# One VectorE instruction for three closing half rows, GpSimd's last products into tiles already stored, and new order tables for every engine

## The chip, the core and the metric

The kernel runs on one core of one Trainium2 chip. The metric is the device time of one execution in microseconds (us), lower is better. One execution was also taken with the hardware profiler, and every duration below comes from that trace.

## What is computed

One decoder layer with four head groups, 1024 tokens by 1024 channels, in float32. Cut to what matters here:

```python
h = rms_norm(x, norm_g)
p = h @ w_in                                  # 1024 x 3652
y_fox = forgetting_attention(fq, fk, fv, log_f)
y_sb  = stick_breaking_attention(sq, sk, sv)
y_rw  = rwkv7_time_mix(rw, ...)               # a recurrence over the tokens
y_lru = rg_lru(lx, ...)
y = concat(y_fox*silu(fg), y_sb*silu(sg), y_rw*silu(rg), y_lru*silu(lg))
x = x + y @ w_out
return x * rsqrt(mean(x*x) + eps) * final_g   # the final RMSNorm
```

## The kernel before, in words

TensorE (PE in the profile) is the engine that matters: float32 products are made from float32r pieces (a rounded high part and a low rest), so each product of the projections and of the output is three matmuls of 128x512 (names `xh`/`xl`, `wh`/`wl`, `woh`/`wol`).

The program runs in stages that overlap:

- From 0 to about 300 us: the input projections (`pj_...`, line L402, later L989) and, woven between their matmuls, the RWKV group. Its recurrence is cut into chunks of 64 tokens, and each chunk is a chain across engines (L758): `px` on PE, `X` on ACT, `pu` and `py` on PE, `UV` on DVE, `ph` on PE, and so on. Between two links of this chain PE works on projection matmuls, which thus are the filling of the gaps. Earlier, a low-rank gate of RWKV runs through `rbc` (a row of scales is spread over the partitions), tanh on ACT and the small matmuls `pw`/`pa` (L498, L501), and a norm over heads through `pn` (L518).
- From about 300 to 470 us: the stick-breaking attention (names ending in `sb`) with the remaining projections as filling.
- From about 470 to 594 us: the forgetting attention (`fox`). Scores `zfox` (L1174) go into PSUM banks; VectorE (DVE) reads a bank, adds the bias and writes `atfox` with a running maximum `mx` (L1213); `nb` (L1218, L1219) is the negated maximum; ScalarE (ACT) takes the exponential (L1222) and scales it by the reciprocal of the sum (L1226, L1229); PE transposes (`ptfox`, L1246), ACT and DVE split the result into `PHfox` and `PLfox` (L1251, L1252), and PE multiplies with the values `VS` (`avfox`, L1256). The filling here is the output projection over three of the four head groups: for row tile `tt` and column half `n` a PSUM tile `po` takes 18 matmuls (L1351) of the weights `woh`/`wol` and of `yc`, the mixed outputs of two row tiles, and one DVE addition (L1353) writes `ac = po + xt`. GpSimd (POOL) issues the loads of `yc` (L1403, two of 768 KB for each pair of tiles), of the residual rows `xt` (L1409, 256 KB each, two buffers), of raw weights `wor` (L1331), and the stores `p_fv` (L1006) of the value projections. In `po<tt><n>` and `xt<tt><n>` the two figures are tile and column half; `yc<g><n>` serves the tiles 2g and 2g+1.
- From 594 us on: the fox group's part of the output (`pofx`, 96 matmuls, L1351), added to `ac` by DVE, and the final RMSNorm by row tile in `out_norm`, in the order 6, 7, 4, 5, 2, 3, 0, 1: ACT squares a half row with its sum (L1359), DVE and ACT make the reciprocal root `rs` (L1361 to L1374), POOL multiplies the half row by the weight `fg` (L1381) in place, and ACT (L1385) or, for three last half rows, DVE (L1383) scales it by `rs`; then it is stored (L1386).

The order of work on each engine is written out by hand: `ORDERS` holds for each of the five engines a list of instruction numbers, and `in_order` lays each engine's stream out by it. A DMA is queued by the engine that issues it: POOL's DMAs go out in the order of POOL's stream, between its own instructions. Each engine works off its stream strictly in order, so an instruction that waits holds all behind it.

Of the kernel before, what the change touches and what calls it, by code (L numbers as in the profile page):

```python
# [13 lines left out]
ALU = mybir.AluOpType  # L14
# [28 lines left out]
for _name, _w in (  # L43
# [171 lines left out]
def tile_hybrid_trunk(ctx: ExitStack, tc: tile.TileContext, a, dbg=None):  # L215
    nc = tc.nc
# [12 lines left out]
    HELD = {}  # L229
# [850 lines left out]
    QB = 2  # L1080
# [274 lines left out]
    def out_norm(w1, op, ac, fg, tt, last):  # L1355
# [21 lines left out]
        for n in range(2):  # L1377

            cs = slice(n * HS, (n + 1) * HS)
# [171 lines left out]
```

## Time and profile before

| | us |
|---|---|
| median of 3 runs | 627.14 (626.68 to 628.49) |
| the profiled execution | 629.03 |
| its span in the trace | 627.1 |
| PE busy | 608.5 (97%), 4060 records |
| DVE busy | 489.8 (78%) |
| ACT busy | 390.7 (62%) |
| POOL busy | 200.8 (32%) |
| granted TensorE clock, mean | 0.992 |

The span is the trace's time from the first to the last event; the execution's own time is 1.9 us longer. Read the table so: PE is busy nearly all the time, so a microsecond is won only where PE idles or runs at a lower clock, or behind its last matmul at 617.14 us.

### The profile page before, as it was taken

Reading aid. Unit: us, or ns where it says so; the run is one execution under the profiler, and the core shown is the slowest. Engines: PE = TensorE matmul, PEld = TensorE weight load, DVE = VectorE, ACT = ScalarE, POOL = GpSimd, SP = SyncE. Lnnn points to the kernel's source line nnn. Section 1 sums busy time; section 2 is a strip of 40 time slices with the busy share of each in tenths; the row PEclk is TensorE's granted clock in tenths of the full one; section 3 lists DMA queues with packets and bytes.
Section 4 is the critical chain, followed back from the end, with each engine's and each line's share of the span. In section 5 each row is a group of like instructions: output and inputs, shape, how many; then the busy total and the mean of one; then the engine's idle time right before and its main releaser. Section 6 shows DMA issues by size and latency. Waiting matters only on the chain.

```text
span 627.1 us, 11831 instructions
## 1 busy us (share of the span) xinstructions
PE 608.5 (97%) x4060; PEld 494.9 (79%) x4060; DVE 489.8 (78%) x1131; ACT 390.7 (62%) x722; POOL 200.8 (32%) x328
## 2 busy tenths in 40 slices
PE   8999999999999999999999999999999999999993
PEld 6867777778876687777888888879997788888882
DVE  6598687998996796978866988888774776857687
ACT  6797948451013378797534776567764657766575
POOL 2231421313113675444343220400223222322175
PEclk9999999999999999999999999999999899999997
DMA  8873766527351336721998665355498867763225
GB/s 288 305 220 87 193 176 152 143 101 183 108 165 62 103 99 222 241 100 71 254 300 270 202 211 159 134 169 168 143 273 298 261 207 248 256 197 135 84 102 201
DMA packets 86403, 114.35 MB, mean 182 GB/s; under 512 B 38151, under 2 KB 57927, under 8 KB 86344
## 3 DMA queue, kind: packets, MB, share of 16 engines
q1 hardware_dynamic: 69112, 57.81, 31.0%
q0 software_dynamic: 16656, 55.23, 26.1%
q8 instruction: 32, 0.52, 0.3%
q10 hardware_dynamic: 576, 0.56, 0.3%
q14 instruction: 27, 0.22, 0.1%
HBM read 79.31 MB, written 33.21 MB: 179 GB/s over the span
## 4 chain that ended last, share of the span: by engine, by line
PE 65%; DVE 13%; ACT 7%; DMA 7%; issue 6%; POOL 2%; SPq 1%; DVEq 0%; ACTq 0%; POOLq 0%
PE po L1351 9%; PE pj_fk L402 4%; PE pofx L1351 4%; PE pj_sg L402 4%; PE pj_fq L402 3%; PE pj_sq L402 3%; PE pj_rg L402 3%; PE pj_fg L402 3%; PE zsb L1174 3%; PE avfox L1256 3%; PE pj_v L402 3%; PE zfox L1174 2%; PE avsb L1256 2%; PE ptfox L1246 2%; DMA xr<-in_xT_dram 2%
## 5 line engine op out<-in xcount | busy, mean ns | idle before, releaser
L1351 PE MATMUL po<-woh,yc 128*128 128x512 f32 x192 | 69.6, 412 | 0.0
L1190 DVE TENSOR_TENSOR_SCAN atsb<-kp,atsb 128x128 f32<-128x128 f32 (+7 forms) x32 | 43.4, 1362 | 5.1 <-ACT atsb L1188 4.9
L1351 PE MATMUL po<-wol,yc 128*128 128x512 f32 x96 | 39.8, 414 | 0.0
L1222 ACT ACTIVATE atfox<-atfox,nb 128x128 f32<-128x128 f32 (+7 forms) x32 | 24.6, 770 | 23.9 <-DVE nb L1219 12.7
L1351 PEld LDWEIGHTS po<-woh,yc 128*128 128x128 f32 x192 | 34.8, 192 | 2.9
L1187 ACT ACTIVATE kp<-zsb 128x512 f32<-128x512 f32 (+3 forms) x48 | 23.6, 491 | 17.5 <-PE zsb L1174 17.0
L1252 DVE TENSOR_TENSOR PLfox<-ptfox,PHfox 128x512 fp32r<-128x512 f32 (+1 forms) x40 | 25.4, 636 | 10.4 <-ACT PHfox L1251 9.8
L1252 DVE TENSOR_TENSOR PLsb<-ptsb,PHsb 128x512 fp32r<-128x512 f32 (+1 forms) x40 | 25.1, 630 | 8.3 <-ACT PHsb L1251 7.5
L1251 ACT ACTIVATE PHsb<-ptsb 128x512 fp32r<-128x512 f32 (+1 forms) x40 | 22.1, 555 | 10.8 <-PE avsb L1256 5.9
L1251 ACT ACTIVATE PHfox<-ptfox 128x512 fp32r<-128x512 f32 (+1 forms) x40 | 21.9, 548 | 11.1 <-PE avfox L1256 9.7
L1174 PE MATMUL zsb<-KSsb,Q 128*128 128x512 f32 (+3 forms) x96 | 28.6, 357 | 0.0
L1174 PE MATMUL zfox<-KSfox,Q 128*128 128x512 f32 (+3 forms) x96 | 25.6, 349 | 2.2 <-DVE mx L1213 2.2
L1229 ACT ACTIVATE atfox<-atfox,sm 128x128 f32<-128x128 f32 (+7 forms) x32 | 23.4, 767 | 0.7 <-DVE sm L1226 0.7
L1188 ACT ACTIVATE atsb<-zsb 128x512 f32<-128x512 f32 (+3 forms) x48 | 23.4, 488 | 0.0
L749 POOL TENSOR_TENSOR Hp<-UV,PC 64x128 f32<-64x128 f32 x32 | 16.6, 518 | 21.3 <-DVE UV L796 17.6
L1174 PEld LDWEIGHTS zfox<-KSfox,Q 128*128 128x128 f32 x96 | 17.8, 191 | 6.2 <-DVE mx L1213 2.6
L1246 PE MATMUL ptsb<-ident,atsb 128*128 128x128 f32 x144 | 22.2, 272 | 0.4 <-DVE PLsb L1252 0.4
L1381 POOL TENSOR_TENSOR ac<-ac,fg 128x512 f32<-128x512 f32 x16 | 20.7, 1324 | 5.6 <-ACT ot L1359 5.6
L1213 DVE CUSTOM_DVE_ANT_0 atfox<-zfox,Fb 128x512 f32<-128x512 f32 (+3 forms) x40 | 20.9, 524 | 2.0 <-PE zfox L1174 1.8
L1246 PEld LDWEIGHTS ptfox<-ident,atfox 128*128 128x128 f32 x144 | 18.2, 140 | 5.5
L1246 PE MATMUL ptfox<-ident,atfox 128*128 128x128 f32 x144 | 22.2, 272 | 0.0
L1256 PE MATMUL avsb<-PLsb,VS 128*128 128x256 f32 x80 | 20.1, 286 | 0.9 <-DVE PLsb L1252 0.7
(547 smaller groups left out, 2161.6 us busy)
## 6 DMA issues: line engine op xcount, KB each, us to landing
yc<-yx_d POOLq DMA_DIRECT2D x16, 768.0 KB, 6.9
xn<-in_x_dram SPq DMA_DIRECT2D x8, 512.0 KB, 5.3
Q<-p_sq SPq DMA_DIRECT2D x64, 64.0 KB, 3.4
Q<-p_fq SPq DMA_DIRECT2D x64, 64.0 KB, 3.6
xt<-in_x_dram POOLq DMA_DIRECT2D x16, 256.0 KB, 6.1
out_dram<-ac SPq DMA_DIRECT2D x15, 256.0 KB, 2.1
xr<-in_xT_dram SPq DMA_DIRECT2D x6, 512.0 KB, 9.0
wor<-in_w_out_dram SPq DMA_DIRECT2D x9, 256.0 KB, 3.8
```

The source lines that it names most:

```text
L402: mm = nc.tensor.matmul(out[0:ww.shape[-1]], ww, xx[hf][:, k], start=(k == 0 and xx is xh and ww is wh), stop=(k == KT - 1 and ww is wl))
L1174: ((hi - c) / 2400, nc.tensor.matmul(z[:, c - lo:hi - lo], q, k, start=j == 0, stop=j == len(ops) - 1))
L1187: nc.scalar.activation(kp[:, lo:hi], z[:, 0:hi - lo], AF.Sigmoid, scale=-0.125)
L1188: nc.scalar.activation(at[:, lo:hi], z[:, 0:hi - lo], AF.Sigmoid, scale=0.125)
L1190: nc.vector.tensor_tensor_scan(rv, kp[:, 0:n][:, ::-1], rv, 0.0, op0=ALU.mult, op1=ALU.add)
L1222: exp = nc.scalar.activation(At[qb][:, 0:n], At[qb][:, 0:n], AF.Exp, bias=nb[:, qb:qb + 1], scale=0.125, accum_out=sm_[:, 0, qb:qb + 1])
L1229: nc.scalar.activation(At[qb][:, 0:n], At[qb][:, 0:n], AF.Copy, scale=sm_[:, 1, qb:qb + 1])
L1246: T.append((P / 1200, nc.tensor.transpose(pt[:, col:col + P], At[qb][:, (2 * m + j) * P:(2 * m + j + 1) * P], ident)))
L1251: nc.scalar.activation(PH[:, 0:w], pt[:, 0:w], AF.Copy)
L1252: nc.vector.tensor_tensor(PL[:, 0:w], pt[:, 0:w], PH[:, 0:w], op=ALU.subtract)
L1256: V.append(((c1 - c0) / 2400, nc.tensor.matmul(av[:, q0:256], VS[:, 2 * m + j, :], pp[:, c0:c1], start=m == 0 and j == 0 and pi == 0, stop ...
L1351: mm = nc.tensor.matmul(po, y, w, start=i == 0, stop=i == len(ops) - 1)
```

## The change

`out_norm` multiplies the three half rows that VectorE finishes (half 1 of tile 3, half 1 of tile 0, half 0 of tile 1) by `rs` and by `fg` in one scalar_tensor_tensor, where before GpSimd multiplied by `fg` and VectorE scaled by `rs`. GpSimd thus has 13 products in place of 16. For the tiles 0 and 1 the results, of both engines, go into the tiles `ac4` and `ac5`, which were stored before, rather than in place.

All tables in `ORDERS` are new. The table of PE is the same from about its 2260th instruction on (from about 340 us); the tables of DVE, ACT, POOL and SP differ in places throughout. Since DVE's table is one line longer, a line number of the changed kernel is one more than that of the same code before.

```diff
     "PE": (
-        "0-9 14-25 38-49 26-37 50-93 10-13 94-109 150-161 110 111 162-197 112 198-221 258-283 117-123 125-131 124 "
+        "0-9 14-25 38-49 26-37 50-87 10-13 88-103 110 111 104-109 150-175 112 176-219 117-123 125-131 124 132-136 "
...
@@ -1377,11 +1378,11 @@
         for n in range(2):
 
             cs = slice(n * HS, (n + 1) * HS)
-            yn = ac[tt][:, cs]
-            nc.gpsimd.tensor_tensor(yn, yn, fg[:, cs], op=ALU.mult)
+            y, yn = ac[tt][:, cs], ac[tt + 4 if tt < QB else tt][:, cs]
             if n in last:
-                HELD[f"scaled{tt}"] = nc.vector.tensor_scalar_mul(yn, yn, rs)
+                HELD[f"scaled{tt}"] = nc.vector.scalar_tensor_tensor(yn, y, rs, fg[:, cs], op0=ALU.mult, op1=ALU.mult)
             else:
+                nc.gpsimd.tensor_tensor(yn, y, fg[:, cs], op=ALU.mult)
                 HELD[f"scale{tt}"] = nc.scalar.activation(yn, yn, AF.Copy, scale=rs)
             (nc.scalar if tt == 1 and n in last else nc.sync).dma_start(a["out"][tt * P:(tt + 1) * P, cs], yn)
```

Three places of the new order follow, each as it stood and as it stands.

**POOL around the first residual row, at about 467 to 475 us.** The names: `FM11` is a mask tile, `yc10` the mixed outputs of the tiles 2 and 3, `xt00` and `xt10` the residual rows of tile 0 and 1, `p_fv` the stored value projections, `wor51` and `wor61` raw output weights. Before:

```order
L1331 DMA wor51_5641<-in_w_out_dram 128x512
L1331 DMA wor61_5647<-in_w_out_dram 128x512
L1006 DMA p_fv_2720<-sp_fv6_2950 128x512
L1197 AFFINE_SELECT FM11_6115<-Fb1_5960 128x256
L1403 DMA yc10_5582<-yx_d_128 128x6x256 x2
L1409 DMA xt00_5538<-in_x_dram 128x512
L1006 DMA p_fv_2720<-sp_fv7_2980 128x512
L1409 DMA xt10_5560<-in_x_dram 128x512
```

After:

```order
L1007 DMA p_fv_2720<-sp_fv6_2950 128x512
L1198 AFFINE_SELECT FM11_6115<-Fb1_5960 128x256
L1410 DMA xt00_5538<-in_x_dram 128x512
L1404 DMA yc10_5582<-yx_d_128 128x6x256 x2
L1410 DMA xt10_5560<-in_x_dram 128x512
L1007 DMA p_fv_2720<-sp_fv7_2980 128x512
```

The load of `xt00` stands ahead of the two large loads of `yc10` where it stood behind them; the two raw weights left this place (they now follow the load of `xt50`), and `xt10` changed places with the last store.

**DVE around the first addition of `po` and `xt`, at about 480 to 488 us.** The names: `nb11` is the negated maximum for which ACT's exponentials of `atfox12` and `atfox13` wait; `atfox04` and `atfox05` are scores on their way out of the PSUM banks `zfox`; `mx` is a running maximum, `sm` a sum of exponentials. Before:

```order
L1353 TENSOR_TENSOR ac0_5527<-po00_5540,xt00_5538 128x512
L1218 TENSOR_REDUCE nb11_6134<-mx11_6119 128x2
L1219 TENSOR_SCALAR nb11_6134<-nb11_6134 128x2
L1201 MEMSET mx12_6263 128x6
L1226 RECIPROCAL sm_11_6121<-sm_11_6121 128x2
L1213 ISA atfox04_6187,mx02_6184<-zfox040_6188,Fb0_5950 128x512
...
L1252 TENSOR_TENSOR PLfox010_6090<-ptfox010_6084,PHfox010_6089 128x512
```

After:

```order
L1219 TENSOR_REDUCE nb11_6134<-mx11_6119 128x2
L1220 TENSOR_SCALAR nb11_6134<-nb11_6134 128x2
L1202 MEMSET mx12_6263 128x6
L1262 TENSOR_TENSOR ypfox00_5963<-avfox10_6031,ypfox00_5963 64x256
L1214 ISA atfox04_6187,mx02_6184<-zfox040_6188,Fb0_5950 128x512
...
L1253 TENSOR_TENSOR PLfox010_6090<-ptfox010_6084,PHfox010_6089 128x512
L1354 TENSOR_TENSOR ac0_5527<-po00_5540,xt00_5538 128x512
```

The addition stood ahead of `nb11` and of the reading of the next score bank and now stands behind both; the reciprocal, which waits for the exponentials, no longer stands ahead of `atfox04`.

**PE in the second chunk of the RWKV chain, at about 185 to 188 us.** `pu`, `py` and `ph` are links of the chain, `pj_sq` the projection that fills. Before:

```order
L758 MATMUL py_3341<-UV_256,TR_259 64x64 x2
L402 MATMUL pj_sq_0_1571<-xh_126,wh_sq_1_1566 128x512
L402 MATMUL pj_sq_0_1571<-xl_127,wh_sq_1_1566 128x512
L402 MATMUL pj_sq_0_1571<-xh_126,wl_sq_1_1567 128x512
L402 MATMUL pj_sq_0_1571<-xh_126,wh_sq_1_1566 128x512
L402 MATMUL pj_sq_0_1571<-xl_127,wh_sq_1_1566 128x512
L758 MATMUL ph_3385<-UV_256,BKT_260 64x64 x4
```

After:

```order
L759 MATMUL py_3341<-UV_256,TR_259 64x64 x2
L403 MATMUL pj_sq_0_1571<-xl_127,wh_sq_0_1560 128x512
L403 MATMUL pj_sq_0_1571<-xh_126,wl_sq_0_1561 128x512
L403 MATMUL pj_sq_0_1571<-xh_126,wh_sq_1_1566 128x512
L759 MATMUL ph_3385<-UV_256,BKT_260 64x64 x4
```

Three filling matmuls stand between `py` and `ph` where five stood. Of the first eight chunks, five now have just three there; before, one had.

199 rows, old and new, of the table ORDERS are left out of this document.

## The prediction

> **What bounds the kernel now.** The page comes first: who is busy, and what clock TensorE was granted in 40 slices of the span.
>
> ```profile
> PE 608.5 (97%) x4060; PEld 494.9 (79%) x4060; DVE 489.8 (78%) x1131; ACT 390.7 (62%) x722; POOL 200.8 (32%) x328
> PEclk9999999999999999999999999999999899999997
> ```
>
> PE leaves 18.6 us of 627.1 idle, so a change in the order of the other engines pays only where PE idles or is slowed, or behind PE's last matmul. The clock falls once in mid program, in slice 32 (486 to 502 us), and otherwise only in the last slice. Next, the table of PE's waits, with total, count and longest:
>
> ```profile
> PE zfox L1174 <- DVE mx L1213: 2.2, 1, 2.2
> PE pn L518 <- ACT N L516: 0.8, 1, 0.8
> PE ph L758 <- DVE UV L783: 0.7, 3, 0.3
> PE avsb L1256 <- DVE PLsb L1252: 0.7, 1, 0.7
> ```
>
> One wait stands out, 2.2 us before a score matmul, and it lies just where the clock falls. The chain of waits between 440 and 500 us says what it hangs on (start, duration, what):
>
> ```profile
> 473.34 10.46 DMA xt<-in_x_dram
> 483.83 0.69 DVE ac L1353
> 484.83 1.42 ACT atfox L1222 x4
> 486.44 0.59 DVE atfox L1213
> 487.09 1.22 PE zfox L1174 x2
> ```
>
> The load of the first residual row took 10.46 us. DVE's addition waited for it, and behind the addition stood the maximum `nb11` for ACT's exponentials, behind these (through the reciprocal) DVE's reading of a score bank, and behind that PE's next scores. The timelines of POOL, DVE and PE give the pieces; the bracket at a row's end is the idle time before it and what ended it:
>
> ```profile
> 467.77 1.08 POOL L1331 DMA_DIRECT2D wor<-in_w_out_dram  x2
> 471.66 1.70 POOL L1403 DMA_DIRECT2D yc<-yx_d  x2 [1.20 <-PE zfox L1174]
> 473.34 0.56 POOL L1409 DMA_DIRECT2D xt<-in_x_dram  x1
> 483.83 0.69 DVE L1353 TENSOR_TENSOR ac<-po,xt 128x512 f32<-128x512 f32 x1 [3.16 <-DMA xt<-in_x_dram]
> 484.49 0.40 PE L1351 MATMUL po<-wol,yc 128*128 128x512 f32 x1
> 487.09 1.22 PE L1174 MATMUL zfox<-KSfox,Q 128*128 128x512 f32 x2 [2.20 <-DVE mx L1213]
> ```
>
> The residual row (256 KB) was queued right behind two loads of 768 KB each, and all three landed at about the same time. What the wait costs is seen in stretches of 10 us, where the fields are busy time and number of instructions by engine, then clock, DMA share and GB/s:
>
> ```profile
> 480.00:490.00 10.00, 7.76 (x35) 6.34 (x36) 5.23 (x19) 4.18 (x10) 1.92 (x4) 0.85 0.80 282
> 490.00:500.00 10.00, 10.00 (x59) 8.58 (x58) 7.63 (x30) 5.63 (x11) 2.68 (x5) 0.98 0.80 263
> 500.00:510.00 10.00, 10.00 (x58) 8.51 (x57) 6.26 (x23) 6.94 (x15) 2.25 (x3) 1.00 0.58 185
> ```
>
> **Part 1, the load and the addition moved apart.** POOL now queues `xt00` ahead of the two `yc10` loads, and two raw weights (512 KB) have left the queue in front of them. DVE's addition now stands behind `nb11` and behind the reading of `zfox040` and `zfox041`. Either move alone would do: nothing that PE's scores need stands behind the addition any more. Cost of the wait: 2.2 us idle; the clock, (1 − 0.85) + (1 − 0.98) over 10 us each, 1.7 us; and some 0.2 us between the last matmul's start (484.49 + 0.23 for one at full speed) and the 2.2 us counted. Sum 4.1 us. The counts agree: 35 records against 58.5 in the two stretches behind it, at 10/58.5 = 0.17 us each, is 4.0 us. I take −4.1.
>
> The clock is the disputed piece. The Trainium skill, "TensorE: Matmul & The Clock Gate", Part 1 (the HAM clock gate), has TensorE's clock halved only after an idle window of about 3.4 us, so an idle time of 2.2 us should cost itself alone, and the term would be −2.4. The trace differs: 0.85 was granted in the stretch of a 2.2 us wait, and the two matmuls after it show 1.22 us for a pair. The measurement decides.
>
> What is late next? The addition now waits for nothing that PE needs until a PSUM bank of `po` is wanted again; it stands one instruction behind `PLfox010`, and that is where the slack was anyway. The loads are closer. PE reads the second `yc10` load at the row shown first here; the other rows are the landing times of that load and of `p_fv7`, which is queued behind `xt10` now:
>
> ```profile
> 490.24 0.45 PE L1351 MATMUL po<-woh,yc 128*128 128x512 f32 x1
> yc<-yx_d POOLq DMA_DIRECT2D x1, 768.0 KB, 10.3
> p_fv<-sp_fv POOLq DMA_DIRECT2D x1, 256.0 KB, 10.2
> ```
>
> Issued at about 473.3, the load landed at about 483.6. Without the stall PE wants it at 490.24 − 4.1 = 486.1. `xt00` ahead of it adds 256 KB at the queue's speed, 1792 KB from 471.66 to 483.83 or 147 KB/us, so 1.7 us: 485.3 at worst, 0.8 us in time, and the absent weights help. I take no new wait; if this cover fails, part of the stall is back (first rival).
>
> **Part 2, the tail.** Rows of the chain and the timeline after the last matmul:
>
> ```profile
> 617.16 0.69 DVE ac L1353
> 619.08 2.66 POOL L1381 TENSOR_TENSOR ac<-ac,fg 128x512 f32<-128x512 f32 x2 [1.08 <-ACT ot L1359]
> 619.48 2.55 DVE L1383 TENSOR_SCALAR ac<-ac,rs 128x512 f32<-128x512 f32 x2
> 621.95 0.14 DVE L1371 TENSOR_SCALAR rsq<-rsq 128x1 f32<-128x1 f32 x1
> 622.50 0.21 DVE L1374 TENSOR_SCALAR rs<-rsq,rs 128x1 f32<-128x1 f32 x1
> 622.82 0.49 DVE L1383 TENSOR_SCALAR ac<-ac,rs 128x512 f32<-128x512 f32 x1
> L337 DVE SCALAR_TENSOR_TENSOR xl<-xr,pc,xh x16: 733/745/752, 4.8 to 40.7; 128x512 fp32r<-128x512 f32 x16
> ```
>
> Two scalings took 2.55 us beside POOL's last two products, the third 0.49 us alone; tile 1's `rs`, at 622.71 the last thing that is waited for, stood behind the two. After: POOL's products need not wait for the squares, since they no longer overwrite what these read, and one fewer stands in the end, so its last (1.33 us) can run from the addition's end, 617.85, to 619.2. The combined instruction is priced by `xl`, of the same shape and operation: 0.745 us. Two of them stand ahead of tile 1's `rs`: 2 × 0.745 = 1.49 against 2.55, a gain of 1.06. Given back: ACT now scales both halves of tile 2 ahead of the last square, which so starts about 0.2 us later; tile 1's mean and root now stand behind the first combined instruction, where they ran beside it, some 0.3 us; and the third is 0.745 against 0.49, 0.26 us. Together 1.06 − 0.76 = 0.3. I take −0.3. Bounds: −0.6 if the late square is hidden; +0.5 if the first two are slowed as the two scalings were (1.28 each, 0.53 more apiece) and the rest stays.
>
> **Part 3, PE's table up to 340 us.** PE's work is the same, only its sequence is not. Two places change by sums that rows can bound.
>
> ```profile
> 28.15 0.58 ACT L367 ACTIVATE rst_bc<-rbc 128x512 f32<-128x512 f32 x1
> 31.08 0.63 ACT L478 ACTIVATE sm<-sm 32x512 f32<-32x512 f32 x1 [0.29 <-DVE sm L476]
> 32.72 0.69 PE L498 MATMUL pw<-sm,wa 32*128 32x512 f32 x1
> 36.91 0.69 ACT SW L503
> 43.06 1.10 PE pn L518 x2
> 44.16 0.93 PE pj_v L402 x4
> ```
>
> `pw` moves 18 matmuls ahead, `rbc`, from which its input comes, 6 matmuls. At 0.23 us each (0.93 for four, the last row) `pw` is wanted at 28.5 and `rbc` is done 1.4 us earlier. ACT's steps from the start of `rst_bc` to the end of the tanh took 3.56 us, of which 1.9 were their own work, so the tanh ends between 28.7 and 30.3: a new wait of 0.2 to 1.8 us. I take 0.65, near the closed-up end, since the new table of ACT puts `rst_bc` and the tanh ahead of the splitting work that stood between them. `pn`, 0.8 us late before, moves 22 matmuls ahead, 5.1 us. Its input comes from `pw` by way of `SW`, which ACT took up only 3.1 us after `pw` had ended (32.72 + two matmul pairs, 33.85), behind splitting work. The new table puts `SW` right behind the tanh and two splits. So its input comes 4.2 us earlier with `pw`, up to 3.1 us earlier by this and 0.65 later by the new wait: 6.6 against the 5.1 + 0.8 it needs. I take −0.8 (bound: 0).
>
> In the RWKV chain the filling between `py` and `ph` shrinks to three matmuls in five of the first eight chunks, from one. The first two chunks before show both cases (three and five fillings):
>
> ```profile
> 182.83 0.23 PE L758 MATMUL py<-UV,TR 64*64 64x64 f32 x2
> 184.13 0.45 PE L758 MATMUL ph<-UV,BKT 128*64 128x64 f32 x8 [0.19 <-DVE UV L783]
> 186.73 0.22 PE L758 MATMUL py<-UV,TR 64*64 64x64 f32 x2
> 188.24 0.45 PE L758 MATMUL ph<-UV,BKT 128*64 128x64 f32 x8
> ```
>
> With three, `ph` came 1.30 us after `py` and had waited; with five, 1.51 us and no wait. Two matmuls fewer save 0.21 rather than 0.46 us, so 0.25 us is lost each time. Four more such chunks: +1.0 (bounds 0 to +2, if the later chunks, whose filling is uneven, lose as much).
>
> **The sum.** −4.1 − 0.3 + 0.65 − 0.8 + 1.0 = −3.55 us. The profiled execution (629.03, its span 627.1 and 1.9 around it) is 0.3% above the median 627.14, so the same difference is set against the median: 623.6.
>
> **The rivals.**
>
> *The stall comes back through another load.* If the second `yc10` load lands more than 0.8 us beyond my worst case, or the values behind `p_fv7` are late, PE stands again near 486 to 497 us. For it: the queue was full (10.2 to 10.5 us to landing). Against: 512 KB left it. Between a quarter and all of the 4.1 us returns; at three quarters 623.6 + 3.1 = 626.7, no change. Chance 0.15.
>
> *The clock was not the stall's.* If the lower clock of 480 to 500 us has another cause than the stall and comes anyway, 1.7 us stay: 625.3, on the bound of no change. For it: one stall is one case. The Trainium skill's rule on idle windows, cited above, would have it so. Against: no other mid-program slice of the row PEclk shows it. Chance 0.07.
>
> *Slower: the chain's links become the bound.* There are 15 gaps between `py` and `ph` and about as many between `px` and `pu` and between `py` and `px`, 45 in all. PE's table pulls the chain forward by thinner fillings throughout, so each gap may now be a wait of 0.25 us, with PE idle while its filling is pushed to where nothing needs it. The point of no gain is 14 such waits beyond my four (3.55 / 0.25), that of over 0.3% slower 22 (with 1.9 us more). With 25: 623.6 + 6.2 = 629.8. For it: the chunk rows above, and the short fillings of the new order. Against: several new gaps hold five to eight fillings, and those of three are barely under the floor. Chance 0.12.
>
> **How the numbers follow.** My forecast has 0.66. A measurement of this kernel can tell about 0.3%, 1.9 us, from no change. Faster by more than that is the forecast alone, 0.66; the first two rivals are within it, 0.15 + 0.07 = 0.22; slower is the third, 0.12. The range: the low end takes each term's better bound, −4.1 − 0.6 + 0.2 − 0.8 + 0 = −5.3, and the `avsb` wait of 0.7 gone besides: 621.1. The high end takes in the first rival with the whole stall back (627.7) and a part, 0.3, of the tail's worse bound: 628.0. Outside lie the third rival and a little below.
>
> **What would show it.** In the profile after: DVE's addition of `po00` with no wait for `xt`; the row PE zfox <- DVE mx gone from the table of waits; 58 records or so and a clock of 1.00 in the stretch that begins 5 us or so before 490; `pw` with a wait of about 0.65 and `pn` with none; waits of `ph` for UV numbering some seven; three combined instructions of 0.75 us, and the last `rs` about 5 us after the last matmul. I am wrong if the stretch is clean and the time is still above 626: then waits before 340 us took it back; or if PE stands again for a load of POOL's queue.

## The result, and the profile after

Slower, where faster was forecast: a median of 631.18 us over 12 runs (629.59 to 632.87) against 626.98 over 12 runs of the kernel before (625.24 to 631.14). The ratio is 1.0058 with an interval of 1.0040 to 1.0076, or +3.6 us (2.5 to 4.8). The forecast was 623.6 us with a range up to 628.0. The profiled execution took 629.86 us, its span 628.2, where before's took 629.03 and 627.1.

The page of the kernel after, busy time and clock:

```profile
PE 607.1 (97%) x4060; PEld 492.4 (78%) x4060; DVE 494.4 (79%) x1131; ACT 388.4 (62%) x721; POOL 195.7 (31%) x325
PEclk9999999999999999999999999999999999999998
```

The dip of the clock in mid program is gone. The stretches where the stall was (busy time and count by engine, clock, DMA share, GB/s) and VectorE's addition there, which no longer shows an idle time in front of it:

```profile
480.00:490.00 10.00, 10.00 (x56) 8.48 (x55) 7.42 (x32) 7.23 (x17) 1.66 (x4) 1.00 0.95 321
490.00:500.00 10.00, 10.00 (x58) 8.49 (x57) 7.33 (x25) 5.52 (x11) 3.22 (x5) 1.00 0.80 264
```

```profile
489.52 0.69 DVE L1253 TENSOR_TENSOR PLfox<-ptfox,PHfox 128x512 fp32r<-128x512 f32 x1
490.13 0.68 DVE L1354 TENSOR_TENSOR ac<-po,xt 128x512 f32<-128x512 f32 x1
```

So 114 matmul records stand in these 20 us where before had 35 + 59 = 94, worth some 20 × 10/58.5 = 3.4 us. PE's table is the same in both kernels here, so the same matmuls can also be timed, which is closer. Between each of these two pairs of rows lie the same 30 matmuls, before with the wait among them:

```profile
483.92 0.49 PE L1246 MATMUL ptfox<-ident,atfox 128*128 128x128 f32 x3
...
493.31 0.60 PE L1246 MATMUL ptfox<-ident,atfox 128*128 128x128 f32 x4
```

```profile
489.52 0.49 PE L1247 MATMUL ptfox<-ident,atfox 128*128 128x128 f32 x3
...
494.97 0.49 PE L1247 MATMUL ptfox<-ident,atfox 128*128 128x128 f32 x3
```

They took 9.4 us before and 5.45 after: 3.9 us were won in this pair of traces. The 55 matmuls ahead of them took 11.4 us before and 10.65 after, another 0.8 us, for which the prediction has no term.

The loss is in the table of PE's waits (total, count, longest):

```profile
PE px L759 <- POOL Hp L750: 1.5, 1, 1.5
PE px L759 <- DVE UV L797: 1.3, 5, 0.3
PE lg L1057 <- DVE xs L1051: 1.2, 1, 1.2
...
PE ph L759 <- DVE UV L784: 1.1, 3, 0.5
PE pu L759 <- ACT X L768: 1.0, 1, 1.0
...
PE pq L710 <- DVE WQ L696: 0.6, 1, 0.6
...
PE yt L825 <- DVE Y L817: 0.2, 1, 0.2
```

All of these lie between 181 and 300 us, in and beside the RWKV chain: 6.9 us. Before had there, with the `ph` row shown in the prediction (0.7), these two, 1.6 us in all:

```profile
PE px L758 <- DVE UV L796: 0.5, 3, 0.2
...
PE pu L758 <- ACT X L767: 0.4, 1, 0.4
```

New: 5.3 us. The busy time of the same 119 us agrees, 117.13 us before and 111.92 after, 5.2 less, and the same 1526 matmuls, which begin at 150 and end at 303 us in before, took 153.0 us there and 158.3 in after. In these rows the third field is PE's:

```profile
181.00:300.00 119.00, 117.13 (x1263) 88.70 (x1262) 94.33 (x193) 78.28 (x123) 58.45 (x92) 1.00 0.42 136
```

```profile
181.00:300.00 119.00, 111.92 (x1208) 82.49 (x1207) 102.26 (x202) 71.13 (x114) 57.71 (x90) 1.00 0.36 122
```

A smaller loss lies ahead of that stretch: PE's 519th matmul, behind the same 518 in both kernels, starts at 110.27 us before and at 111.32 us after.

The tail, in the timeline after the last matmul:

```profile
618.57 0.69 DVE L1354 TENSOR_TENSOR ac<-pofx,ac 128x512 f32<-128x512 f32 x1
...
620.91 0.73 DVE L1383 SCALAR_TENSOR_TENSOR ac<-ac,rs,fg 128x512 f32<-128x512 f32 x1
...
622.18 0.74 DVE L1383 SCALAR_TENSOR_TENSOR ac<-ac,rs,fg 128x512 f32<-128x512 f32 x1
...
623.39 0.75 DVE L1383 SCALAR_TENSOR_TENSOR ac<-ac,rs,fg 128x512 f32<-128x512 f32 x1
```

From the last addition's start to the span's end are 628.2 − 618.57 = 9.63 us, before 627.1 − 617.16 = 9.94: 0.31 us won.

### The profile page after: what moved, and what is told of

Same layout as the page of the kernel before. It is cut to its first block, busy times and chain, and to the rows that moved or that the text cites. A ratio compares the mean times of both kernels' runs of the same rounds, so it can differ in the third digit from the quotient of the medians.

```text
span 628.2 us, 11807 instructions
## 1 busy us (share of the span) xinstructions
PE 607.1 (97%) x4060; PEld 492.4 (78%) x4060; DVE 494.4 (79%) x1131; ACT 388.4 (62%) x721; POOL 195.7 (31%) x325
## 4 chain that ended last, share of the span: by engine, by line
PE 64%; DVE 15%; DMA 7%; issue 5%; ACT 5%; SPq 2%; POOL 1%; DVEq 0%; ACTq 0%; POOLq 0%
PE po L1352 10%; PE pj_fk L403 4%; PE pj_sg L403 4%; PE pj_fq L403 3%; PE pofx L1352 3%; PE pj_fv L990 3%; PE pj_fg L403 3%; PE zsb L1175 3%; PE avsb L1257 3%; PE pj_rg L403 3%; PE avfox L1257 3%; PE zfox L1175 3%; PE pj_sv L990 3%; PE ptfox L1247 2%; PE ptsb L1247 2%
## 5 line engine op out<-in xcount | busy, mean ns | idle before, releaser
L1223 ACT ACTIVATE atfox<-atfox,nb 128x128 f32<-128x128 f32 (+7 forms) x32 | 24.6, 770 | 16.2 <-DVE nb L1220 9.4
L1247 PEld LDWEIGHTS ptsb<-ident,atsb 128*128 128x128 f32 x144 | 17.6, 140 | 3.8 <-DVE PLsb L1253 0.6
```

The costliest lines, as they stand in the source:

```text
L1223: exp = nc.scalar.activation(At[qb][:, 0:n], At[qb][:, 0:n], AF.Exp, bias=nb[:, qb:qb + 1], scale=0.125, accum_out=sm_[:, 0, qb:qb + 1])
L1247: T.append((P / 1200, nc.tensor.transpose(pt[:, col:col + P], At[qb][:, (2 * m + j) * P:(2 * m + j + 1) * P], ident)))
```

## The experiments

The theory at the start: the late part of the tables and the tail win what was forecast, and the early part loses more than that, at links of the chain with thin filling (the third rival). The other: the late part wins less than forecast. Most kernels here put before's tables and after's together. `E[a:b]` stands for the entries a to b of an engine's table; the cuts lie where both tables have issued the same instructions, at about 151, 211 and 344 us (PE 650, 1043, 1740; DVE 263, 414, 594; ACT 131, 151, 279; POOL 93, 125, 217; SP 67, 104, 182). PE's own third cut comes earlier, at about 313 us: its two tables are the same from about the 1730th entry on, at 311 us of before, and not only from the 2260th as was said above. Ratios are to the kernel before on the same chip; 0.001 is 0.63 us.

**The late part and the early part, each alone (`e1_late_part`, `e2_early_part`).**

```diff
-"PE": after[:]
+"PE": before[:1740] + after[1740:]     # e1, and so for each engine
+"PE": after[:1740] + before[1740:]     # e2
```

> Tables of before up to about 344 us on every engine, tables and tail of after behind that. Chain theory (what was lost lies before 344 us, where PE's table pulls the RWKV chain forward; what was forecast behind it was won): the stall before the scores at 484 us is gone and the tail is 0.3 us shorter, so 2.5 to 4.4 us faster than before, 622.6 to 624.5. Rival (the part behind 344 us brought nothing in most executions, since their stall is smaller than the profiled one's, or a new late transfer costs it): within 1 us of before.

> The reverse: tables of after up to about 344 us, tables and tail of before behind that. Chain theory: PE's added idle time before 344 us (6.5 us in the trace of after against that of before) with the stall and the tail of before kept: 5.5 to 7.5 us slower than before, 632.5 to 634.5. Rival: no more than the 3.6 us that the whole change lost, 627 to 630.6.

Measured: `e1` 624.62 us, ratio 0.9956 (0.9934 to 0.9977), −2.8 us (−4.1 to −1.4). `e2` 633.70 us, 1.0081 (1.0044 to 1.0117), +5.1 us (2.8 to 7.3). The two sum to +2.3, near the +3.6 of both together. The late part is a gain, smaller than the 4.4 us forecast; the early part is the whole loss. The waits of `e2` between 181 and 300 us sum to 6.8 us, those of `e1` to 1.6.

**The addition moved alone (`e3_dve_add_later`).** One instruction of VectorE goes behind `PLfox010`; the load stays where it was.

```diff
-L1353 TENSOR_TENSOR ac0<-po00,xt00
 L1218 TENSOR_REDUCE nb11<-mx11
 ...
 L1252 TENSOR_TENSOR PLfox010<-ptfox010,PHfox010
+L1353 TENSOR_TENSOR ac0<-po00,xt00
```

> Before with one DVE instruction moved: the first addition of po and xt stands behind PLfox010, as after has it; POOL's queue is as before. Stall theory: the load may be as late as it likes, PE no longer stands for it: 2.4 us faster if the clock is held in any case, 4.1 if the lower clock came with the stall, so 622.9 to 624.6. Rival (the load itself, not the addition's place, is what counts): PE stands elsewhere for the same time, within 1 us of before.

Measured: 627.11 us, 0.9980 (0.9948 to 1.0013), −1.3 us (−3.3 to +0.8). The row of `zfox` waiting for `mx` is gone, and the 30 matmuls around it took 5.9 us in this trace, against 9.4 before. But a gain of 4.1 us lies outside the interval: the move is worth 3.3 us at the most, and no gain at all is within it too. The load moved alone was not tried.

**The tail alone, twice (`e4_tail_alone`, `e8_tail_again`).** The new `out_norm`, with before's tables but for their ends (from PE 3478, DVE 987, ACT 606 and SP 340 on, and POOL's last products).

```diff
-"DVE": before[:]
+"DVE": before[:987] + after[987:]
+HELD[f"scaled{tt}"] = nc.vector.scalar_tensor_tensor(yn, y, rs, fg[:, cs], op0=ALU.mult, op1=ALU.mult)
```

> Before with the edit of out_norm and the new tables from about 600 us on alone. Forecast: 0.3 us faster, not to be told from no change. Rival (the products out of place or the three-operand instruction cost the end): 0.5 us slower or more. From the last addition to the span's end 9.94 us in before, 9.6 expected.

> The kernel of e4 once more, on another call's chip, since its ratio there (0.9956, 0.9922 to 0.9989) was more than the 0.3 us that its trace shows behind the last addition. If 0.3 us is all: a ratio of 0.9995, the interval with 1 in it or near it. If the tail is worth more: 0.9956 again.

Measured: first 626.24 us, 0.9956 (0.9922 to 0.9989), then 626.62 us, 0.9992 (0.9965 to 1.0018). The same kernel gave −2.8 and −0.5 us; the forecast of −0.3 stands inside the second interval only, and two results that far apart cannot size so small a term. The trace of `e8` has something else to tell. Its wait and its stretch at the stall, with the old order there:

```profile
PE zfox L1174 <- DVE mx L1213: 1.0, 1, 1.0
```

```profile
480.00:490.00 10.00, 8.48 (x46) 6.64 (x46) 6.45 (x23) 4.19 (x10) 2.63 (x4) 1.00 0.83 286
```

The wait was 1.0 us where before's profiled execution had 2.2, and the clock did not fall. In `e4` the same wait was 0.3 us, and 48 records stood in the stretch.

**The stall made longer (`e7_xt_behind_more`).** On the kernel before, 512 KB more stand in POOL's queue between the `yc10` loads and `xt00`.

```diff
-L1331 DMA wor51<-in_w_out_dram
-L1331 DMA wor61<-in_w_out_dram
 ...
 L1403 DMA yc10<-yx_d x2
+L1331 DMA wor51<-in_w_out_dram
+L1331 DMA wor61<-in_w_out_dram
 L1409 DMA xt00<-in_x_dram
```

> Before, with the two raw weights wor51 and wor61 (512 KB) queued between yc10 and xt00, so that the first residual row lands later. Stall theory: at 147 KB/us the row lands up to 3.5 us later and PE's scores wait for it through DVE's addition and ACT's exponentials: 2 to 4 us slower than before, the idle time between 470 and 500 us up by as much, and with an idle time of over 2 us a lower clock there. Rival (the load is not what the scores wait for): no change.

Measured: 627.84 us, 1.0021 (0.9996 to 1.0045), +1.3 us (−0.3 to 2.8). Its waits and its stretch:

```profile
PE zfox L1174 <- DVE mx L1213: 2.5, 1, 2.5
```

```profile
480.00:490.00 10.00, 7.51 (x33) 5.99 (x33) 5.40 (x17) 4.18 (x10) 2.31 (x4) 0.83 0.80 260
```

Here the wait and the fallen clock stand together again, but the wait is only 0.3 us longer than in before's profiled execution, and 2 us of loss or more was expected. The row was not later either: its load took 9.60 us here and 10.46 in before, so that the 3.5 us from the rate of 147 KB/us did not come. (The two weights stood ahead of `yc10` before, so all that is queued ahead of the row is the same number of bytes.) The experiment thus shows the way from the load to PE and from the wait to the clock once more, as the prediction read it; it does not show that more in the queue makes the stall longer.

**The chain's links first (`e5_links_first`).** On the kernel after, seven links on VectorE and one on ACT go ahead of the one or two instructions of other groups that held them, such as:

```diff
 L784 COPY UV<-pu x2
+L797 TENSOR_TENSOR UV<-ph,Hp
 L852 TENSOR_TENSOR yo<-yo,sg
 L852 TENSOR_TENSOR ly<-ly,lyh
-L797 TENSOR_TENSOR UV<-ph,Hp
```

> After, with links of chains moved ahead of other work on their engine at eight places: DVE's copies and sums UV ahead of WT, fe, sp_sq, sp_sk and yo (183 to 281 us), its transpose WQ ahead of yo (234 us), its step xs ahead of yo (236 us), and ACT's copy X ahead of sg and two weight splits (260 us). PE's table stays. Held-link theory (PE waits because a link stands behind other work on DVE or ACT): the waits at these eight places, 6.3 us in the trace of after, go for the most part; 3 to 6 us faster than after, that is 1 to 3 us faster than before or equal to it. Thin-filling theory (too few matmuls between the links, as predicted): PE waits just as long, within 1 us of after, 3 to 4 us slower than before.

Measured: 629.12 us, 1.0045 (1.0023 to 1.0066), against 1.0058 of the kernel after: no difference that the intervals can tell. Its waits:

```profile
PE px L759 <- DVE UV L797: 2.8, 5, 0.8
PE bkt L616 <- ACT UV L608: 1.7, 2, 1.3
PE pu L759 <- ACT X L768: 1.5, 1, 1.5
...
PE lg L1057 <- DVE xs L1051: 0.8, 1, 0.8
```

The wait of `px` for `Hp` and that of `pq` are gone, and as much stands at other links: 6.9 us between 181 and 300 us, exactly as much as without the moves. So single instructions in the wrong place are not the cause. That VectorE and ACT have too much to do there is one reading; the runs below test it.

**Thicker filling (`e6_fills_wide`).** On the kernel after, the five thin gaps between `py` and `ph` get five filling matmuls in place of three, taken from the longest gap.

```diff
 L759 MATMUL py<-UV,TR x2
 L403 MATMUL pj_sq ... (three)
+L403 MATMUL pj_sq ... (two more)
 L759 MATMUL ph<-UV,BKT x4
```

> After, with five filling matmuls in place of three between py and ph in the five early chunks that have three, taken from the end of that stretch; nothing else changed. Thin-filling theory: 0.25 us won at each, 1.2 us faster than after. Held-link theory: three of the five had no wait and the work that holds the other two moves along, so less than 0.6 us either way.

Measured: 645.74 us, 1.0301 (1.0268 to 1.0334). It failed as a test. Its largest wait is new and has nothing to do with the gaps; PE stands before a projection until VectorE has read out an earlier result (`sp_sq`, L969):

```profile
PE pj_sk L403 <- DVE sp_sq L969: 9.8, 2, 5.5
```

It does show how tightly the tables fit: ten fillings of 0.23 us put forward cost 0.0243 (1.0301 − 1.0058) or 15 us against the kernel after. Without an experiment the kernel after answers part of the question. Two of its `py`–`ph` pairs with three fillings:

```profile
185.99 0.23 PE L759 MATMUL py<-UV,TR 64*64 64x64 f32 x2
187.04 0.45 PE L759 MATMUL ph<-UV,BKT 128*64 128x64 f32 x8
...
193.89 0.22 PE L759 MATMUL py<-UV,TR 64*64 64x64 f32 x2
194.94 0.45 PE L759 MATMUL ph<-UV,BKT 128*64 128x64 f32 x8
```

`ph` came 1.05 us after `py` with no wait. So the 1.30 us that the prediction took for the least a link can take was not the least; that link had waited for something else, and what that was is not shown.

**Where in the early part (`e9_middle_s2`, `e10_middle_s3`).** After's tables for one stretch alone, in the kernel before: from 151 to 211 us, which holds the first eight chunks with their thin filling, and from 211 to 344 us.

```diff
-"PE": before[:]
+"PE": before[:650] + after[650:1043] + before[1043:]     # e9
+"PE": before[:1043] + after[1043:1740] + before[1740:]   # e10
```

> Before with the tables of after on all engines between 151 and 211 us alone (the first eight chunks of the chain). If the loss lies in the order of this stretch itself: PE's added idle time of after between 180 and 230 us, 2.5 us, is found again, and the time is 1.5 to 3 us above before. If the loss comes only from what the stretches ahead of and behind it shift (rival): within 1 us of before.

> Before with the tables of after on all engines between 211 and 344 us alone (the other seven chunks, the late parts of RWKV and the RG-LRU group). If the loss lies in the order of this stretch itself: the 2.7 us that after lost between 230 and 300 us are found again, with the long waits for Hp, xs and X of 1.0 to 1.5 us each: 2 to 3.5 us slower than before. Rival, as for e9: within 1 us of before.

Measured: `e9` 628.49 us, 1.0023 (0.9996 to 1.0050); `e10` 631.28 us, 1.0060 (1.0032 to 1.0088), as much as the whole change. The waits of `e10`, whose line numbers are two less than after's:

```profile
PE px L757 <- POOL Hp L748: 1.5, 1, 1.5
PE lg L1055 <- DVE xs L1049: 1.2, 1, 1.2
PE px L757 <- DVE UV L795: 1.2, 5, 0.3
...
PE pu L757 <- ACT X L766: 1.0, 1, 1.0
...
PE pq L708 <- DVE WQ L694: 0.6, 1, 0.6
```

They are after's, one by one: with `yt` 5.7 us between 181 and 300 us, where after has 6.9 and before 1.6. `e9` has 2.6 us. Its interval alone would leave room for a loss of up to 3 us, but the same 646 matmuls of its stretch took 63.0 us in it and 62.95 before. The thin filling is innocent of most of the loss, which is made after 211 us. What is different there? VectorE's work. Grouped by line from 211 to 300 us (count, then busy time and mean ns of one), three groups that are no links of the RWKV recurrence, before:

```profile
L1050 DVE SCALAR_TENSOR_TENSOR xs<-xb,pc,xs 128x512 f32<-128x512 f32 x12 | 10.7, 895 | 2.0 <-ACT xs L1048 1.7
L611 DVE TENSOR_TENSOR BK<-BK,PCt 128x1024 f32<-128x1024 f32 x2 | 2.7, 1366 | 0.4 <-PE pg L565 0.4
...
L851 DVE TENSOR_TENSOR yo<-yo,sg 128x512 fp32r<-128x512 f32 x2 | 1.4, 692 | 0.3 <-ACT sg L850 0.3
```

and in `e10`:

```profile
L1049 DVE SCALAR_TENSOR_TENSOR xs<-xb,pc,xs 128x512 f32<-128x512 f32 x12 | 11.8, 982 | 0.2
L610 DVE TENSOR_TENSOR BK<-BK,PCt 128x1024 f32<-128x1024 f32 x2 | 4.0, 1995 | 0.0
L850 DVE TENSOR_TENSOR yo<-yo,sg 128x512 fp32r<-128x512 f32 x2 | 2.9, 1448 | 0.0
```

The same 16 instructions take 18.7 us in place of 14.8, and the idle time ahead of them is gone. The timelines of the kernel after show one such case, DVE, then POOL, then PE:

```profile
278.70 1.74 DVE L852 TENSOR_TENSOR yo<-yo,sg 128x512 fp32r<-128x512 f32 x1
280.37 0.68 DVE L852 TENSOR_TENSOR ly<-ly,lyh 128x512 fp32r<-128x512 f32 x1
281.07 0.61 DVE L797 TENSOR_TENSOR UV<-ph,Hp 64x128 f32<-64x128 f32 x2
```

```profile
278.63 1.26 POOL L1063 TENSOR_TENSOR lg<-lg,xs 128x512 f32<-128x512 f32 x1 [0.66 <-issue]
281.44 1.23 POOL L750 TENSOR_TENSOR Hp<-UV,PC 64x128 f32<-64x128 f32 x2 [1.54 <-DVE UV L797]
```

```profile
281.83 0.45 PE L759 MATMUL px<-UV,GM 128*64 128x64 f32 x8 [1.46 <-POOL Hp L750]
```

`yo` started just behind GpSimd's `lg` and took 1.74 us where its like, `ly`, takes 0.68 with GpSimd idle. Behind it stood the link `UV`, behind that GpSimd's `Hp`, behind that PE's `px`: 1.46 us. The Trainium skill, "SBUF — State Buffer", section "SBUF: two separate sides", says that VectorE and GpSimd share one pair of ports, and that of a VectorE instruction with two SBUF inputs and a GpSimd instruction that reads SBUF the one that starts first holds it until it ends, the other standing still. The rows agree: `lg` ends at 279.89, and 0.55 us later, a little less than the 0.68 us of `ly`, `yo` is done.

**VectorE's other work cut to a sliver (`e11_sliver_before`, `e12_sliver_after`).** In both kernels, five operations that are no links of the recurrence work on 8 of 512 columns; their number and order stay, most of their work is left out. One of them is `xs`, for which PE's `lg` waits, so that wait is shortened directly.

```diff
-nc.vector.tensor_tensor(yf, yf, gt, op=ALU.mult)
+nc.vector.tensor_tensor(yf[:, 0:8], yf[:, 0:8], gt[:, 0:8], op=ALU.mult)
```

> Control. Before, with five kinds of DVE work beside the chain cut down to 8 of 512 columns (left out: most of the group norm's bias and gate, of the low parts of the two recurrent outputs, of the convolution and of the low part of the split projections). Order and number of instructions stay. DVE's bystander work falls by some 20 us between 180 and 300 us. Held-link theory: PE's waits in the chain (about 2 us) go for a part, 0 to 2 us faster than before. Thin-filling theory: no change.

> After with the same work left out. Held-link theory: the waits at which a link stood behind such work (Hp at 281, xs at 238, WQ at 235, UV at 210 and 270 us) go, so PE's surplus of idle time over e11 between 180 and 300 us falls from 5.2 to under 2.5 us and the time is 3 to 5 us below after. Thin-filling theory: the surplus stays at 4 to 5 us, and the time is above e11 by as much as after is above before.

Measured: `e11` 626.86 us, 0.9990 (0.9968 to 1.0013); `e12` 626.25 us, 0.9986 (0.9961 to 1.0011). The cut is worth 0.6 us to before and 4.5 us to after (1.0058 − 0.9986). The waits from 181 to 300 us are 3.0 us in `e12` and 2.5 in `e11`, of which 1.3 is for a transfer. So the loss needs this work on VectorE, but the experiment cannot say whether for its amount or for its meeting GpSimd.

**GpSimd's work cut (`e13_pool_sliver_after`, `e14_pool_sliver_before`).** VectorE's work is whole; GpSimd's gate products get 8 of 512 columns, and a quarter of the masks `GM` is made.

```diff
-nc.gpsimd.tensor_tensor(gt, gt, sg, op=ALU.mult)
+nc.gpsimd.tensor_tensor(gt[:, 0:8], gt[:, 0:8], sg[:, 0:8], op=ALU.mult)
-        pattern=[[0, 4], [1, 2], [1, 64]], channel_multiplier=-1)
+        pattern=[[0, 1], [1, 2], [1, 64]], channel_multiplier=-1)
```

> After, with GpSimd's gate products of the two recurrent groups cut to 8 of 512 columns and its triangular masks GM to a quarter (left out: the rest of those products and masks). VectorE's work is whole and in after's order. Port theory (VectorE's instructions are held while GpSimd reads): VectorE's instructions of this stretch get back the 4 us that they lost, and PE's surplus of idle time over e14 between the first and the last px of the chain falls from 5.1 us to under 2.5 us; 2.5 to 5 us faster than after. Rival (VectorE has too much work between the links, whatever GpSimd does): the surplus stays at 4 us or more.

> Control for e13: before with the same GpSimd work left out. Port theory: VectorE little faster there, 0 to 1.5 us faster than before. Rival: no change.

Measured: `e13` 626.93 us, 1.0002 (0.9985 to 1.0019); `e14` 628.63 us, 1.0020 (0.9994 to 1.0045). The cut is worth 3.5 us to after and gains nothing for before, whose interval has 1 in it. The three groups of VectorE in `e13`:

```profile
L1051 DVE SCALAR_TENSOR_TENSOR xs<-xb,pc,xs 128x512 f32<-128x512 f32 x12 | 9.1, 758 | 0.8 <-ACT xs L1049 0.5
L612 DVE TENSOR_TENSOR BK<-BK,PCt 128x1024 f32<-128x1024 f32 x2 | 2.5, 1264 | 0.0
...
L852 DVE TENSOR_TENSOR yo<-yo,sg 128x512 fp32r<-128x512 f32 x2 | 1.5, 732 | 0.0
```

13.1 us for what took 18.7, with the same instructions in the same order. Of the waits (4.0 us in `e13`, 1.5 in `e14`), `lg` for `xs` and `pq` for `WQ` are gone and `px` for `Hp` is 0.4; `px` for `UV` (1.2), `ph` (1.1) and `pu` (0.9) are as they were. The surplus of waits is 2.5 us, just at the bound that was set. The same 880 matmuls, which lie between 213 and 303 us in before, say it more closely: 90.0 us before, 94.8 in after, 91.5 in `e13` and 89.8 in its control `e14`, so that the surplus falls from 4.8 to 1.7. By the waits, the meeting of VectorE and GpSimd makes 1.1 + 1.2 + 0.6 = 2.9 us of the 5.3 new ones, by the matmuls 3.1 of 4.8. This shows that GpSimd's work costs VectorE the time; whether by the shared ports or in another way, these runs do not tell. Of the rest, some 0.8 at `px` falls with VectorE's own amount of work (0.4 in `e12`), 0.4 is left of the wait for `Hp`, 0.6 is at `pu`, 0.4 at `ph` and 0.2 at `yt`. ACT's splits stand ahead of the `X` for which `pu` waits, but `e5` moved `X` ahead of some of them and the wait was 1.5 us, so that cause is open.

**The parts that cost nothing (`e15_costless_parts`).** After's tables from 151 to 211 us and from 344 us on, with the new `out_norm`; before's elsewhere.

```diff
-"PE": after[:]
+"PE": before[:650] + after[650:1043] + before[1043:1740] + after[1740:]
```

> Before with the tables of after between 151 and 211 us and from 344 us on, and the edit of out_norm: the parts that cost nothing or win. If the parts add up: as e1, 0.9956 of before or a little less (623.5 to 625).

Measured: 624.42 us over 9 runs, 0.9957 (0.9942 to 0.9972), −2.7 us (−3.6 to −1.8). With `e1` (0.9956) it is the best version, faster than both kernels; and since it differs from `e1` by the stretch with the thin filling alone, that stretch costs nothing that can be measured.

## Why the prediction was wrong

- **The failed step that turned the sign: "+1.0 (bounds 0 to +2)" for PE's table up to 340 us.** The waits of the chain's stretch grew by 5.3 us, and the early part alone measured +5.1 (2.8 to 7.3). The prediction looked at PE's table and the number of fillings between two links. The loss came from the tables between 211 and 344 us (`e10`, all engines together). The new waits there are waits for VectorE, GpSimd and ACT, whose tables that part never costed: links stand behind other work, and that work itself is slower beside GpSimd, which makes some 3 us of the 5 (`e13`). The row of `yo` against `ly` could not be seen before the run, but something like it could: two scalings of VectorE took 2.55 us beside GpSimd's products where one alone took 0.49, in the rows of Part 2, and that was priced for the tail alone. In the trace of before, `xs` took 895 ns on the mean, 754 with GpSimd's work cut (`e14`).
- **The thin filling between `py` and `ph` was no cause.** The floor of 1.30 us was none (1.05 in the kernel after), `e9` has all the thin gaps and lost no more than its interval can tell, and three waits of `ph` came, not some seven. For PE's fillings behind 211 us no run stands alone, so a share of the 1.7 us that `e13` leaves may be theirs.
- **The stall, −4.1 us: right for the profiled execution, too large as a term.** The wait and the dip went as forecast, 3.9 us in the two profiled executions. But the term was carried over to the median whole, by "the same difference is set against the median". How long the load keeps VectorE waiting changes from run to run: with the old order there, `zfox` waited 2.2 us in before, 2.0 in `e14`, 1.4 in `e9`, 1.0 in `e8`, 0.7 in `e11`, 0.5 in `e2`, 0.3 in `e4` and not at all in `e10`. Against 5.4 us with the new order, the 30 matmuls lost 3.9, 3.9, 2.3, 1.9, 1.6, 1.4, 1.2 and 0.0 us, on the middle 1.7. That before's profiled execution was 1.9 us above its own median was the hint: its surplus was in good part this stall.
- **The clock: right where the wait was long.** `e7` (2.5 us, 0.83) and `e14` (2.0 us, 0.83) show the dip again; at a shorter wait it stayed away (1.4 us in `e9`, 1.00), and the term counted it as certain. The idle window of about 3.4 us in the Trainium skill, "TensorE: Matmul & The Clock Gate", Part 1 (the HAM clock gate), is longer than each of these three waits of 2.0 to 2.5 us that came with a dip.
- **The tail, −0.3: right**, 0.31 us in the traces, with combined instructions of 0.73 to 0.75 us as priced. The timed runs of it alone are too far apart to confirm it. From the last `avfox` matmul to the last matmul of all PE took 23.62 us before and 23.38 after, another 0.24 us won, for which the prediction has no term.
- **`pw` and `pn`, +0.65 − 0.8: wrong in sign, and small.** `pn` has no wait in after; `pw` waits 0.3 us in the tables of `e2` and `e12`, and in after too little to be listed. But `rbc`, which was to be done 1.4 us earlier, started only 0.8 us earlier (24.56 against 25.36) and now waits 0.3 us for VectorE's `dg`: its own input was taken to be there. The same 106 matmuls around all three took 25.0 us before and 25.9 after. In eleven traces with before's tables there they took 24.6 us on the middle (23.9 to 25.8), in six with after's 25.6 (25.0 to 26.0). So about 1.0 us was lost where 0.15 was to be won; the other gaps are too short for the table of waits, and their cause is open. In five of the eleven (`e1`, `e7`, `e9`, `e14`, `e15`) `pn` does not wait with before's tables either, so its 0.8 us was not there to be won in every run.
- **The third rival** had the sign, the stage and nearly the size (629.8), at 0.12. Its mechanism, thin fillings at 45 gaps, did not happen, so that its nearness is luck.

The terms as measured are −1.7 (the stall), −0.8 (the matmuls ahead of it), −0.6 (the tail and PE's last part), +1.0 (`pw` and `pn`) and +5.3 (the chain), together +3.2 us, where the timed runs have +3.6 (2.5 to 4.8). Of the difference to the forecast, 4.3 us come from the chain, 2.4 from the stall and 1.15 from `pw` and `pn`; the two terms that were missing take back 1.1. Which engine's table between 211 and 344 us does the harm by itself was not tried: the tables of two engines taken from different kernels there wait for each other in a circle.

## What to carry to other kernels

Before a wait read in one execution is priced, set that execution against the median and look for the same wait in other executions: a wait that ends on a DMA is a spread, not a number. When tables of all engines are new, cost the engines that feed the bottleneck too: list what stands ahead of each link of a serial chain, and which instructions of GpSimd run beside VectorE's instructions with two inputs. A large change of order is best taken apart by stretches of time; here two of its four stretches, with the tail, were worth 2.7 us that the other two hid. Where two traces have issued the same matmuls, time those: a busy share or a table of waits leaves out what is lost in short gaps.

## What the runs showed of the hardware

- The granted clock fell after waits of 2.0, 2.2 and 2.5 us (0.83, 0.85 and 0.83 in the stretch of 10 us), in `e6` after 2.5, 4.3 and 5.5 us (0.83, 0.66 and 0.79), and not after 1.0, 1.4 and 1.5 us (1.00 in `e8`, `e9` and `e5`). The rows of the stretch with the wait of 2.0 us (`e14`) and of that with 1.4 us (`e9`):

```profile
480.00:490.00 10.00, 7.98 (x37) 6.37 (x36) 5.94 (x21) 4.18 (x10) 2.56 (x4) 0.83 0.72 228
```

```profile
480.00:490.00 10.00, 8.26 (x44) 6.49 (x44) 6.00 (x22) 4.57 (x11) 2.92 (x5) 1.00 0.79 262
```

- A VectorE instruction of 128x512 with two inputs, 0.69 us on the mean in before, took 1.45 us where GpSimd worked beside it (`e10`), and one of 128x1024 took 2.00 us where it took 1.26 with GpSimd's work cut (`e13`). No table of waits lists such a loss under its own name; it shows in the mean of the group.
- The landing of one and the same load changed from run to run: VectorE waited 3.16 us for the first residual row in before, 1.23 in `e4` and not at all in `e10`, with the same order of the queue around it.
